# A hybrid decoder step: paced first loads, squares of x on VectorE, and the third norm in pairs of blocks

## The chip, the cores and the metric

The kernel runs on one core of one Trainium2 chip. The metric is the device time of one execution in microseconds (us); the time of a kernel is the median of its runs. Engines are named as in the profile: PE is TensorE (PEld its weight loads), DVE VectorE, ACT ScalarE, POOL GpSimd, SP SyncE, which here only issues DMAs. Lines (L131) are those of the kernel's file before the change.

## The reference

One inference step of one decoder layer, in fp32, for 256 new prompt tokens and 8 x 8 decode tokens, 320 tokens in all, with a model width of 2048:

```python
h    = rms_norm(x, norm_mix_pre)
proj = h @ w_in                       # 2048 x 9248: gate u, v, SSD z, x/B/C, dt
mix  = concat(gate(u, v), ssd(z, xbc, dt)) @ w_out
x    = x + rms_norm(mix, norm_mix_post)
up   = rms_norm(x, norm_ffn_pre) @ ffn_w_up        # 2048 x 11264
f    = (gelu(conv(g)) * conv(u)) @ ffn_w_down      # g, u: the halves of up
x    = x + rms_norm(f, norm_ffn_post)
rms_norm(x, w) = x * rsqrt(mean(x*x) + 1e-6) * w
```

The gate is a spatial gating unit inside chunks of 128 tokens, the SSD a chunked state-space scan; both lie away from the change. The outputs are x, the SSD states and the last rows that the convolutions read.

## The kernel before, in words

**Layout and products.** Activations lie transposed: 128 features of a block on the partitions, 320 tokens (NT) along the row; x has 16 such blocks (KD). Every fp32 product is made of three single-pass products (`accumulate`, L140 to L142): operands are split in a high half (rounded by ScalarE) and a low half (the rest, by VectorE), and high x high, high x low and low x high are summed in PSUM.

**Weights.** `slab` (L110) loads 128 x 1024 weights (two blocks of 128 rows by 512 columns, or four by 256, or one block by 512 as half a slab) by a DMA on SP's queue into `wraw`, casts them on ScalarE to `whi` (L127) and subtracts on VectorE to `wlo` (L131). Each of the three has three buffers, so a load starts when VectorE is done with the slab three before it. `project` (L164) runs 16 blocks of a projection through four PSUM banks. The first projection (the gate's v, L616) has `small=4`: its first four blocks come one at a time (k0 = 0, 1, 2, 3, two to a buffer), then two at a time (k0 = 4, 6, 8, 10), then four. The very first slab is loaded in two cuts (128 and 384 columns) whose products are made by part (L177): four high x high, four high x low, four low x high.

**The start.** TensorE makes ten products of ones (EARLY, L70) that nobody reads, until the first weights are there. x comes by ScalarE's DMA queue (`load_x`, L554) in pieces: block 0 with the scale column, block 1, blocks 2-3, blocks 4-5 at once, and then two blocks each time an odd block has been split (L574). `x_ready` (L565) splits block by block: `h_hi` on ScalarE (L569), `h_lo` on VectorE (L570). A tiny activation (L561) brings ScalarE's table in before its first cast. The first norm's factor does not stand in front of the products: x's squares are taken beside them (`x_squares`, L576), two blocks at a time on ScalarE (L582), and added to a sum (L584), for kt = 2, 4, 6 on GpSimd and for 8 to 14 on VectorE; the factor is multiplied in afterwards.

**The third norm.** After the output projection, `x1_ready` (L1075) makes the new x block by block (L1081, L1082) and splits it, while `project(ffn_w_up, 0, ...)` (L1089) already multiplies four column blocks of the gate half and, with `more`, two of the other half. When the last of the 16 blocks is made (`added[15]`), the squares of all blocks are taken one by one on ScalarE (L301; the first few earlier) and added one by one on VectorE (L302) into `sq3`. TensorE sums them over the partitions with products by ones (`token_sums`, L278), VectorE takes the inverse root in eleven small steps (`rsqrt_of`, L246), TensorE spreads it over the partitions (`spread`, L287), ScalarE copies it to `r3` (L293). In `ffn_up(0)` (L1104, L1146) another column block, `ps_one`, is multiplied meanwhile: two slabs of eight blocks; the sums are asked for behind the first slab, with a priority that draws them as far forward as their data. With `r3` there the six waiting banks and `ps_one` are evicted (L1122, L1123), and the last column block, `ps_other`, takes the first PSUM bank that comes free.

The second norm uses another root, `rsqrt_by_root` (L263): a sum of two parts, ScalarE's square root (L271), VectorE's reciprocal and one refining step.

**What sets the order.** The kernel is written with a scheduler that orders each engine's instructions ahead of time, by priority among those that its own model holds ready; on the chip each engine and each queue then works strictly in that order. `tc.high_priority(offset)` and `first()` raise a priority; `tc.issue_after(ins)` puts what is issued in the block, on the engine of `ins`, behind `ins`. Buffers of a pool that carry one tag are reused in turn, and a writer waits for the readers of what was there.

Of the kernel before, what the change touches and what calls it, by code (L numbers as in the profile page):

```python
# [9 lines left out]
F32 = mybir.dt.float32  # L10
# [3 lines left out]
ALU = mybir.AluOpType  # L14
# [11 lines left out]
NF = DFF // P  # L26
NH = 32
EPS = 1e-6
EARLY = 10
D_COL = 4 * KD + 120 + 8 * NF  # L30
U0, V0, Z0, X0, B0, C0, DT0 = 0, 2048, 4096, 6144, 8192, 8704, 9216

# [2 lines left out]
def hybrid_step(  # L35
# [71 lines left out]

    slab_load, split_after, both = [], [None], []

    def slab(src, half=0, begins=False):  # L110

        n = src.shape[2]
        with tc.high_priority(offset=100000):
            m = n * src.shape[1]
            if not half:
                both[:] = [wp.tile([P, 1024], F32 if i == 0 else F32R, tag=t, name=t, bufs=3) for i, t in enumerate(("wraw", "whi", "wlo"))]
            raw, hi, lo = (t[:, m * half:m * half + m] for t in both)
            cuts = (slice(0, P), slice(P, m)) if begins else (slice(0, m),)
            if begins:
                for o in cuts:  # L120
                    slab_load.append(sp.dma_start(raw[:, o], src[:, 0, o]).ins)
            else:
                slab_load.append(sp.dma_start(raw.rearrange("p (a n) -> p a n", n=n), src).ins)
            late = split_after[-1]
            with tc.issue_after(late[0]) if late else nullcontext(), tc.issue_after(late[1]) if late else nullcontext():
                for i, o in enumerate(cuts):
                    made = act.copy(hi[:, o], raw[:, o]).ins  # L127
                    if begins and i == 0:
                        with tc.issue_after(made):
                            begins()  # L130
                dve.tensor_tensor(out=lo, in0=raw, in1=hi.bitcast(F32), op=ALU.subtract)  # L131

        def block(k, c):
            o = k * n + c * P
            return hi[:, o:o + P], lo[:, o:o + P]
        return block
# [27 lines left out]
    def project(w, c0, evac, width=512, spare=False, late=None, quiet=0, ready=None, small=0, after=None, ahead=1, rate=1, more=None, held=None):  # L164

        nb = width // P
        ps = [misc(f"ps_{c0}_{j}") if spare else mm.tile([P, 512], F32, tag="mm", name=f"ps_{c0}_{j}") for j in range(nb)]
        if more:
            ps += [misc(f"ps_{c0}_{j}") for j in range(nb, nb + 2)]

        def part(src, k0, nk, js):
            wb = slab(src, k0 % 2 if nk == 1 else 0, (lambda: ready(0, 1)) if ready and k0 == 0 and nk == 1 else False)
            by_part = range(1 if ready and k0 == 0 and nk < 4 else 0)
            for k in by_part:
                for i in (0, 1, 2) if nk == 1 else (0, 2, 1):
                    for c, j in enumerate(js):
                        pe.matmul(ps[j][:, :NT], wb(k, c)[i // 2], hT[i % 2][:, k, :], start=i == 0, stop=False)  # L177
            for c, j in enumerate(js):
                for k in range(len(by_part), nk):
                    kt = k0 + k  # L180
                    part_last[:] = [accumulate(ps[j][:, :NT], wb(k, c), hT[0][:, kt, :], hT[1][:, kt, :], kt == 0, kt == KD - 1)]
                if k0 + nk == KD and late is None:
                    evac(j, ps[j])
            if k0 < KD - quiet:
                for _ in range(rate):
                    tick()
        cuts, k0 = [], 0
        if nb == 4:
            while k0 < KD - 4:
                cuts.append((k0, 1 if k0 < small else 2))  # L190
                k0 += cuts[-1][1]
        cuts += [(k, 4) for k in range(k0, KD, 4)]
        there = None

        for cut in cuts[:ahead] if ready else []:
            there = ready(*cut)
        for i, (k0, nk) in enumerate(cuts):
            with tc.issue_after(there or after) if there or after and i > 1 else nullcontext():
                if ready and i + ahead < len(cuts) and (ahead or i):
                    there = ready(*cuts[i + ahead])  # L200
                if nk < 4:
                    part(rows_of(w, k0, nk, c0, 512), k0, nk, range(4))
                    if more and k0 % 4 == 2:
                        if k0 == 2:
                            split_after.append((rooted[-1], low[1]))
                        with tc.issue_after(held[1]):
                            part(rows_of(w, k0 - 2, 4, more, 256), k0 - 2, 4, (4, 5))
                        split_after.append(None)
                else:
                    for h in range(nb // 2):  # L210
                        part(rows_of(w, k0, 4, c0 + 256 * h, 256), k0, 4, (2 * h, 2 * h + 1))
                    if more:
                        part(rows_of(w, k0, 4, more, 256), k0, 4, (4, 5))
        if late is not None:
            late += [(evac, j, p) for j, p in enumerate(ps)]
# [47 lines left out]
    def rsqrt_by_root(rest, ps, scale, rows=P):  # L263

        v = tp.tile([P, 3], F32, tag="rs_v3", name="rs_v")[:rows]
        r = tp.tile([P, 3], F32, tag="rs_r3", name="rs_r", bufs=3)[:rows]
        t = tp.tile([P, 3], F32, tag="rs_t3", name="rs_t")[:rows]
        s = tp.tile([P, 3], F32, tag="rs_s3", name="rs_s")[:rows]
        dve.tensor_scalar(out=v, in0=rest, scalar1=scale, scalar2=EPS, op0=ALU.mult, op1=ALU.add)
        dve.scalar_tensor_tensor(out=v, in0=ps, scalar=scale, in1=v, op0=ALU.mult, op1=ALU.add)  # L270
        rooted.append(act.activation(s, v, AF.Sqrt).ins)  # L271
        dve.reciprocal(r, s)
        dve.scalar_tensor_tensor(out=t, in0=v, scalar=-0.5, in1=r, op0=ALU.mult, op1=ALU.mult)
        dve.tensor_tensor(out=t, in0=t, in1=r, op=ALU.mult)
        rsqrt_ins.append(dve.scalar_tensor_tensor(out=r, in0=t, scalar=1.5, in1=r, op0=ALU.add, op1=ALU.mult).ins)
        return r
# [110 lines left out]
    with ExitStack() as mctx:  # L387
# [153 lines left out]
        with tc.tile_pool(name="gp", bufs=1) as gp:  # L541
# [13 lines left out]
                cs = slice(KD + NT * k if k else 0, KD + NT * (k + n))  # L555
                act.dma_start(flat[:, cs], xT[:, cs])
            with tc.high_priority(offset=300000):
                for k, n in ((0, 1), (1, 1), (2, 2), (4, 2)):
                    load_x(k, n)
                    if k == 1:  # L560
                        act.activation(held, ones[:, 0:1], AF.Square)  # L561

            x_split = []

            def x_ready(k0, nk):  # L565
                with tc.high_priority(offset=100000):
                    for kt in range(k0, k0 + nk):
                        x = xf[:, kt, :]
                        x_split.append(act.activation(hT[0][:, kt, :], x, AF.Copy, scale=pre[:, kt:kt + 1]).ins)  # L569
                        dve.scalar_tensor_tensor(out=hT[1][:, kt, :], in0=x, scalar=pre[:, kt:kt + 1],  # L570
                                                 in1=hT[0][:, kt, :].bitcast(F32), op0=ALU.mult, op1=ALU.subtract)
                        if kt % 2 and kt < 10:
                            with tc.issue_after(x_split[-1]):
                                load_x(kt + 5, 2)  # L574

            def x_squares():  # L576

                yield from repeat(None, 4)
                for kt in range(0, KD, 2):
                    sq = acc[:, kt:kt + 2, :]  # L580
                    with tc.high_priority(offset=100000):
                        act.activation(sq, xf[:, kt:kt + 2, :], AF.Square)  # L582
                    if kt:
                        (pool if kt < 8 else dve).tensor_tensor(out=acc[:, 0:2, :], in0=acc[:, 0:2, :], in1=sq, op=ALU.add)  # L584
                    if kt not in (8, 12):
                        yield
                with first():
# [142 lines left out]
        with tc.tile_pool(name="sd", bufs=1) as sd:  # L730
# [358 lines left out]
            project(ffn_w_up, 0, None, late=up0, ready=x1_ready, after=behind, ahead=1, more=DFF, held=added)  # L1089
            with tc.issue_after(low[2]):  # L1090
                next(rest[1])
            with tc.issue_after(added[15]):
                for kt in range(KD):
                    add_square(sq3, acc[:, kt, :], kt < 1, dve, ("pv", 4))
    x1 = acc


    with tc.tile_pool(name="fp", bufs=1) as fp:
# [5 lines left out]
        def ffn_up(g):  # L1104
# [41 lines left out]
            if g == 0:  # L1146

                ps = misc("ps_one")
                for i in range(2):
                    wb = slab(rows_of(ffn_w_up, 8 * i, 8, DFF + 256, P))  # L1150
                    for k in range(8):
                        kt = 8 * i + k
                        accumulate(ps[:, :NT], wb(k, 0), hT[0][:, kt, :], hT[1][:, kt, :], kt == 0, kt == KD - 1)
                    if i == 0:
                        with first():
                            r = rsqrt_of(token_sums(sq3), 1.0 / D, 3)
                with first():
                    spread(r, r3)
                up0.append((None, 6, ps))
# [208 lines left out]
```

## Time and profile before

| | |
|---|---|
| time, median of 3 runs (lowest to highest) | 1786.09 us (1786.07 to 1788.71) |
| the profiled execution | 1786.56 us |
| its span, first to last instruction | 1784.9 us |
| DVE, ACT, POOL busy | 1191.5, 799.3, 286.7 us |
| moved by DMA | 289.94 MB, 162 GB/s on average |

A profile row of the timeline has the start in us, the duration in us, engine, line, operation, tiles written and read, partitions x elements, and the count of instructions that it joins; in brackets the idle time of the engine before it and what ended it. A row of the waits has who waited, on which line, for what; then us in all, times, and the longest. A row of the chain has start, us and what. A row of one line's instructions has count, then shortest, median and longest in ns, and the first and last start. A row of issues has count, size of one, and the us from issue to landing. The durations of matmuls overlap, since they are pipelined; their starts tell the pace.

### The profile page before, as it was taken

Reading aid. Unit: us, or ns where it says so; the run is one execution under the profiler, and the core shown is the slowest. Engines: PE = TensorE matmul, PEld = TensorE weight load, DVE = VectorE, ACT = ScalarE, POOL = GpSimd, SP = SyncE. Lnnn points to the kernel's source line nnn. Section 1 sums busy time; section 2 is a strip of 40 time slices with the busy share of each in tenths; the row PEclk is TensorE's granted clock in tenths of the full one; section 3 lists DMA queues with packets and bytes.
Section 4 is the critical chain, followed back from the end, with each engine's and each line's share of the span. In section 5 each row is a group of like instructions: output and inputs, shape, how many; then the busy total and the mean of one; then the engine's idle time right before and its main releaser. Section 6 shows DMA issues by size and latency. Waiting matters only on the chain.

```text
span 1784.9 us, 31254 instructions
## 1 busy us (share of the span) xinstructions
PE 1774.2 (99%) x12230; PEld 1743.2 (98%) x12230; DVE 1191.5 (67%) x2077; ACT 799.3 (45%) x1121; POOL 286.7 (16%) x601
## 2 busy tenths in 40 slices
PE   9999999999999999999999999999999999999998
PEld 9999999999999898999999999999999999999998
DVE  7459664556987869677875474756566575656575
ACT  6443455334444445445555333343434343433445
POOL 3104200000431303103121010110101020101004
PEclk9999999999999999999999999999999999999999
DMA  7646544456665565554554555454454545454443
GB/s 231 186 141 200 163 138 154 154 154 184 203 207 185 175 205 179 154 171 146 177 158 149 150 154 153 146 155 150 150 153 152 148 156 151 149 153 153 147 155 107
DMA packets 221699, 289.94 MB, mean 162 GB/s; under 512 B 16368, under 2 KB 151152, under 8 KB 221360
## 3 DMA queue, kind: packets, MB, share of 16 engines
q1 hardware_dynamic: 209824, 268.74, 49.7%
q10 hardware_dynamic: 10016, 14.16, 2.3%
q0 software_dynamic: 1712, 5.05, 0.9%
q8 instruction: 96, 1.57, 0.4%
q14 instruction: 51, 0.42, 0.1%
HBM read 273.08 MB, written 14.82 MB: 161 GB/s over the span
## 4 chain that ended last, share of the span: by engine, by line
PE 94%; issue 2%; DVE 1%; DMA 1%; POOL 0%; ACT 0%; POOLq 0%; SPq 0%; DVEq 0%; ACTq 0%
PE ps L140 20%; PE ps L141 20%; PE ps L142 20%; PE pd L140 10%; PE pd L142 10%; PE pd L141 10%; PE y_ps L946 1%; DMA wraw<-in_w_in 1%; PE yo_ps L851 1%; PE up_ps L868 1%; DVE wlo L131 0%; PE sg L694 0%; PE xt_ps L380 0%; PE vt_ps L600 0%; PE tsum L283 0%
## 5 line engine op out<-in xcount | busy, mean ns | idle before, releaser
L131 DVE TENSOR_TENSOR wlo<-wraw,whi 128x1024 fp32r<-128x1024 f32 (+1 forms) x474 | 582.3, 1229 | 411.0 <-ACT whi L127 409.0
L127 ACT CAST whi<-wraw 128x1024 fp32r<-128x1024 f32 (+1 forms) x475 | 494.8, 1042 | 714.5 <-PE ps L141 416.3
L140 PE MATMUL ps<-h_hi,whi 128*128 128x320 f32 x2520 | 782.5, 311 | 1.4 <-DVE pad L405 0.8
L141 PE MATMUL ps<-h_lo,whi 128*128 128x320 f32 x2520 | 779.1, 309 | 0.8 <-DVE h_lo L570 0.8
L142 PE MATMUL ps<-h_hi,wlo 128*128 128x320 f32 x2520 | 778.6, 309 | 0.2 <-DVE wlo L131 0.2
L140 PEld LDWEIGHTS ps<-h_hi,whi 128*128 128x128 f32 x2520 | 473.5, 188 | 4.8 <-issue 2.8
L141 PEld LDWEIGHTS ps<-h_lo,whi 128*128 128x128 f32 x2520 | 473.7, 188 | 2.8 <-issue 1.1
L142 PEld LDWEIGHTS ps<-h_hi,wlo 128*128 128x128 f32 x2520 | 473.4, 188 | 0.9 <-DVE wlo L131 0.4
L140 PE MATMUL pd<-fhi,whi 128*128 128x320 f32 x704 | 217.4, 309 | 0.0
L141 PE MATMUL pd<-flo,whi 128*128 128x320 f32 x704 | 217.3, 309 | 0.0
L142 PE MATMUL pd<-fhi,wlo 128*128 128x320 f32 x704 | 217.3, 309 | 0.0
L140 PE MATMUL pd<-ohi,whi 128*128 128x320 f32 x448 | 140.7, 314 | 0.0
L142 PE MATMUL pd<-ohi,wlo 128*128 128x320 f32 x448 | 139.1, 310 | 0.0
L141 PE MATMUL pd<-olo,whi 128*128 128x320 f32 x448 | 138.9, 310 | 0.0
L142 PEld LDWEIGHTS pd<-fhi,wlo 128*128 128x128 f32 x704 | 132.3, 188 | 0.0
L141 PEld LDWEIGHTS pd<-flo,whi 128*128 128x128 f32 x704 | 132.3, 188 | 0.0
L140 PEld LDWEIGHTS pd<-fhi,whi 128*128 128x128 f32 x704 | 132.3, 188 | 0.0
L1134 POOL COPY ptf<-pad 128x2 f32<-128x2 f32 x88 | 21.0, 239 | 610.0 <-DVE pad L1122 609.3
L237 DVE TENSOR_TENSOR acc_ffn<-acc_ffn,pd 128x320 f32<-128x320 f32 (+1 forms) x161 | 77.6, 483 | 38.2 <-PE pd L142 36.8
L140 PEld LDWEIGHTS pd<-ohi,whi 128*128 128x128 f32 x448 | 84.2, 188 | 2.0 <-issue 1.1
L141 PEld LDWEIGHTS pd<-olo,whi 128*128 128x128 f32 x448 | 84.2, 188 | 0.4 <-issue 0.2
L142 PEld LDWEIGHTS pd<-ohi,wlo 128*128 128x128 f32 x448 | 84.2, 188 | 0.4 <-issue 0.3
(309 smaller groups left out, 1613.9 us busy)
## 6 DMA issues: line engine op xcount, KB each, us to landing
wraw<-in_ffn_w_up SPq DMA_DIRECT2D x176, 512.0 KB, 3.7
wraw<-in_w_in SPq DMA_DIRECT2D x144, 512.0 KB, 3.8
wraw<-in_ffn_w_down SPq DMA_DIRECT2D x88, 512.0 KB, 3.3
wraw<-in_w_out SPq DMA_DIRECT2D x64, 512.0 KB, 3.4
st<-in_state_ssm SPq DMA_DIRECT2D x32, 256.0 KB, 4.2
out_ssm_state_sample<-st ACTq DMA_DIRECT2D x30, 256.0 KB, 2.9
cs<-dacs_d SPq DMA_DIRECT2D x16, 320.0 KB, 4.5
xr<-in_xT SPq DMA_DIRECT2D x4, 640.0 KB, 4.0
```

The lines of the kernel that those rows point to most:

```text
L127: made = act.copy(hi[:, o], raw[:, o]).ins
L131: dve.tensor_tensor(out=lo, in0=raw, in1=hi.bitcast(F32), op=ALU.subtract)
L140: pe.matmul(ps, whi, xhi, start=first, stop=False)
L141: pe.matmul(ps, whi, xlo, start=False, stop=False)
L142: return pe.matmul(ps, wlo, xhi, start=False, stop=last).ins
L237: added_last[:] = [dve.tensor_tensor(out=acc[:, nb, ts], in0=acc[:, nb, ts], in1=ps[:, ts], op=ALU.add).ins]
L851: pe.matmul(ps_yo[row:row + 32, :256], cms[:, 4 * h + i, :], st[h][:, 256 * r:256 * r + 256], start=i == 0, stop=i == 3, tile_position=(0, ...
L868: made = pe.matmul(ps, bm[:, h], xsp[:, h], start=True, stop=True)
L946: pe.matmul(ps[64 * i:64 * i + 64, cols], w(hl), x(hl, m, cpx), tile_position=(0, 64 * i), **flags)
L1134: pool.tensor_copy(ptf[:, k, :], pad[:, 256:258])
```

## The change

Six edits, at two places. At the start: eight idle products for ten; the slabs of k0 = 3 and k0 = 4 of the first projection get a small VectorE copy into their load buffer, from the first column of the high half of block 0 and of block 1, so that the load waits for that split; the load of x's blocks 2-3 is issued behind the small activation, that of blocks 4-5 behind the split of block 0; all adds of x's squares are VectorE's. At the third norm: the squares are taken of two blocks at a time, into four parts of two buffers that had held x, and added in pairs behind the fourteenth block (`added[13]`), with one last add of the two halves of the pair; the sums are asked for behind the fifth block of `ps_one`, at the earliest; and the inverse root is the one by ScalarE, of one sum (`rest` is None) instead of two.

```diff
-EARLY = 10
+EARLY = 8
...
-    def slab(src, half=0, begins=False):
+    def slab(src, half=0, begins=False, paced=None):
...
+            if paced is not None:
+                dve.tensor_copy(raw[:, 0:1], paced)
             if begins:
...
+        begun = []
+
         def part(src, k0, nk, js):
-            wb = slab(src, k0 % 2 if nk == 1 else 0, (lambda: ready(0, 1)) if ready and k0 == 0 and nk == 1 else False)
+            wb = slab(src, k0 % 2 if nk == 1 else 0, (lambda: ready(0, 1)) if ready and k0 == 0 and nk == 1 else False,
+                      begun[k0 - 3] if small and k0 in (3, 4) else None)
+            if k0 < small:
+                begun.append(wb(0, 0)[0][:, 0:1].bitcast(F32))
...
     def rsqrt_by_root(rest, ps, scale, rows=P):
...
-        dve.tensor_scalar(out=v, in0=rest, scalar1=scale, scalar2=EPS, op0=ALU.mult, op1=ALU.add)
-        dve.scalar_tensor_tensor(out=v, in0=ps, scalar=scale, in1=v, op0=ALU.mult, op1=ALU.add)
+        dve.tensor_scalar(out=v, in0=ps if rest is None else rest, scalar1=scale, scalar2=EPS, op0=ALU.mult, op1=ALU.add)
+        if rest is not None:
+            dve.scalar_tensor_tensor(out=v, in0=ps, scalar=scale, in1=v, op0=ALU.mult, op1=ALU.add)
...
             with tc.high_priority(offset=300000):
-                for k, n in ((0, 1), (1, 1), (2, 2), (4, 2)):
-                    load_x(k, n)
-                    if k == 1:
-                        act.activation(held, ones[:, 0:1], AF.Square)
+                load_x(0, 1)
+                load_x(1, 1)
+                table = act.activation(held, ones[:, 0:1], AF.Square).ins
+                with tc.issue_after(table):
+                    load_x(2, 2)
...
-                        if kt % 2 and kt < 10:
+                        if kt == 0 or kt % 2 and kt < 10:
                             with tc.issue_after(x_split[-1]):
-                                load_x(kt + 5, 2)
+                                load_x(kt + 5 if kt else 4, 2)
...
-                        (pool if kt < 8 else dve).tensor_tensor(out=acc[:, 0:2, :], in0=acc[:, 0:2, :], in1=sq, op=ALU.add)
+                        dve.tensor_tensor(out=acc[:, 0:2, :], in0=acc[:, 0:2, :], in1=sq, op=ALU.add)
...
-            with tc.issue_after(added[15]):
-                for kt in range(KD):
-                    add_square(sq3, acc[:, kt, :], kt < 1, dve, ("pv", 4))
+
+            room = [op.tile([P, 4, NT], F32, tag="xs", name="sq_two", bufs=2) for _ in range(2)]
+            total, *some = [t[:, i:i + 2, :] for t in room for i in (0, 2)]
+            for i, kt in enumerate(range(0, KD, 2)):
+                sq = some[i % 3] if i else total
+                act.activation(sq, acc[:, kt:kt + 2, :], AF.Square)
+                if i:
+                    with tc.issue_after(added[13]):
+                        dve.tensor_tensor(out=total, in0=total, in1=sq, op=ALU.add)
+            dve.tensor_tensor(out=sq3, in0=total[:, 0, :], in1=total[:, 1, :], op=ALU.add)
...
-                        accumulate(ps[:, :NT], wb(k, 0), hT[0][:, kt, :], hT[1][:, kt, :], kt == 0, kt == KD - 1)
-                    if i == 0:
-                        with first():
-                            r = rsqrt_of(token_sums(sq3), 1.0 / D, 3)
+                        made = accumulate(ps[:, :NT], wb(k, 0), hT[0][:, kt, :], hT[1][:, kt, :], kt == 0, kt == KD - 1)
+                        if kt == 4:
+                            with first(), tc.issue_after(made):
+                                r = rsqrt_by_root(None, token_sums(sq3), 1.0 / D)
```

## The prediction

> **What bounds the kernel now.** I read the page first (span, busy shares, chain), then TensorE's own waits, then the timeline around each wait that this change can reach.
>
> ```profile
> span 1784.9 us, 31254 instructions
> PE 1774.2 (99%) x12230; PEld 1743.2 (98%) x12230; DVE 1191.5 (67%) x2077; ACT 799.3 (45%) x1121; POOL 286.7 (16%) x601
> PE 94%; issue 2%; DVE 1%; DMA 1%; POOL 0%; ACT 0%; POOLq 0%; SPq 0%; DVEq 0%; ACTq 0%
> ```
>
> ```profile
> PE ps L141 <- DVE h_lo L570: 0.8, 1, 0.8
> ...
> PE tsum L283 <- DVE sq L302: 0.7, 1, 0.7
> ...
> PE ps L140 <- ACT whi L127: 0.6, 1, 0.6
> ...
> PE ps L142 <- DVE wlo L131: 0.2, 1, 0.2
> ```
>
> TensorE (PE) is busy in 99% of the span and is 94% of the chain. The change removes none of its products but two idle ones, so it can only win where TensorE stands. The second fence is the whole of what it can win by: four waits of 0.8, 0.7, 0.6 and 0.2 us, the first, third and fourth in the first projection, the second at the third norm. Whatever engine gets lighter elsewhere is beside TensorE and worth nothing.
>
> **Part 1: the first products.** The rows are TensorE's and ScalarE's timeline of the first microseconds, then one row of the chain of waits, and the issues with their size and us to landing: the two cuts of the first slab, the third load of x, the fifth slab, and the median of all slabs of this matrix.
>
> ```profile
> 1.13 4.40 PE L70 MATMUL early<-ones 128*128 128x128 f32 x20 [1.13 <-DVE ones L66]
> 3.04 0.20 ACT L561 ACTIVATE held<-ones 128x1 f32<-128x1 f32 x1
> 4.83 0.51 ACT L127 CAST whi<-wraw 128x384 fp32r<-128x384 f32 x1 [0.35 <-DMA wraw<-in_w_in]
> 5.29 0.84 PE L177 MATMUL ps<-h_hi,whi 128*128 128x320 f32 x4
> 6.54 0.75 PE L177 MATMUL ps<-h_hi,wlo 128*128 128x320 f32 x4
> 7.23 0.62 ACT L127 CAST whi<-wraw 128x512 fp32r<-128x512 f32 x1 [1.42 <-DMA wraw<-in_w_in]
> 7.90 0.42 PE L140 MATMUL ps<-h_hi,whi 128*128 128x320 f32 x1 [0.60 <-ACT whi L127]
> 8.88 0.31 PE L140 MATMUL ps<-h_hi,whi 128*128 128x320 f32 x1
> ```
>
> ```profile
> 1.73 5.48 DMA wraw<-in_w_in
> ```
>
> ```profile
> wraw<-in_w_in SPq DMA_DIRECT2D x1, 64.0 KB, 2.5
> wraw<-in_w_in SPq DMA_DIRECT2D x1, 192.0 KB, 3.6
> vt<-in_xT ACTq DMA_DIRECT2D x1, 320.0 KB, 5.6
> wraw<-in_w_in SPq DMA_DIRECT2D x1, 512.0 KB, 7.0
> ...
> wraw<-in_w_in SPq DMA_DIRECT2D x144, 512.0 KB, 3.8
> ```
>
> *Two idle products fewer.* 20 records (two to a product) take 4.40 us, so two products are 4/20 of that, 0.9 us. But only the first of the four real products could use it: the other three need the second cut of the weights, whose split ends at 4.83 + 0.51 = 5.34, and TensorE starts the second of the four at about 5.5 today. Bounds 0 and 0.9; I take **0.1**, next to the split's row.
>
> *The paced loads.* Steady products stand 0.147 apart (four in 0.75 us, the last lasting 0.31: 0.44 / 3). The last of the first block starts at 6.54 + 3 x 0.147 = 6.98; unhindered, the fourth product of the second block would start 0.59 later, at 7.57. It starts at 8.88: **1.30 us lost**, because the second slab, issued at 1.73, lands at 7.21 and is split from 7.23. Its companion is the third load of x (320 KB, issued beside it, 5.6 us to landing). The change issues that one only behind the activation that ends at 3.24 (about 1.5 us later) and after the third slab, holds the fourth slab until the first split, and holds the fifth (512 KB; 7.0 us today) until the second split. So the second slab shares the DMA engines with far less. TensorE wants its high half at about 7.1; the split takes 0.62, so landing by 6.4 wins all. From an issue at 1.73 that is 4.7 us; the two cuts ahead of it landed in 2.5 and 3.6, and with fewer rivals for the bandwidth I expect about 4.3. Bounds 0 (it lands as today) and 1.30; I take **1.1**.
>
> The pacing adds two VectorE copies of 128x1, in the place of a load that used to leave at once. Nearest rows: VectorE's 128x3 operations, 0.16 each. The first waits for the cast of the first cut, which lies before the product at 5.29; until the first split of x VectorE has nothing else to do. The second waits for the second slab's cast; behind it stand that block's own splits, ready at the same moment, so 0.16 is its price. Behind both on SP's queue stand all later slabs: the fourth leaves at about 4, the fifth at about 7. The fifth is wanted three blocks of 12 products after the second block's start, 7.1 + 3 x 1.76 = 12.4; with today's 7.0 us it lands at 14, with the usual 3.8 at 11. This is the new risk (rival A). ScalarE issues the moved x loads in gaps in which it waits for weights anyway.
>
> **Part 2: x's squares.**
>
> ```profile
> 16.27 1.23 DVE L131 TENSOR_TENSOR wlo<-wraw,whi 128x1024 fp32r<-128x1024 f32 x1 [2.41 <-ACT whi L127]
> 17.41 1.56 POOL L584 TENSOR_TENSOR acc_mix<-acc_mix 128x640 f32<-128x640 f32 x1 [11.91 <-ACT acc_mix L582]
> 17.41 2.37 DVE L570 SCALAR_TENSOR_TENSOR h_lo<-vt,h_hi 128x320 fp32r<-128x320 f32 x2
> 18.26 0.31 PE L142 MATMUL ps<-h_hi,wlo 128*128 128x320 f32 x1
> 19.37 0.41 PE L141 MATMUL ps<-h_lo,whi 128*128 128x320 f32 x1 [0.80 <-DVE h_lo L570]
> ```
>
> ```profile
> L570 DVE SCALAR_TENSOR_TENSOR h_lo<-vt,h_hi x16: 537/546/1904, 4.5 to 28.5; 128x320 fp32r<-128x320 f32 x16
> ```
>
> ```profile
> L584 DVE TENSOR_TENSOR acc_mix<-acc_mix x4: 817/821/826, 29.0 to 35.5; 128x640 f32<-128x640 f32 x4
> ```
>
> A GpSimd add and a split of x start together at 17.41; of the 16 such splits the median takes 0.55, the longest 1.90, and it is this one, for while the add runs VectorE crawls. TensorE waits for it: 19.37 - 18.26 is 1.11 between starts instead of 0.147, and 0.1 more at the restart: **1.07 lost**. With no add on GpSimd the split takes 0.55 and the wait has no cause. VectorE takes three adds at 0.82 = 2.5 us, low in priority, and gets back 1.35 from this split alone. Bounds: 1.07 won, or the adds stand in front of splits (rival C). I take **0.9**, since TensorE will come here a microsecond or more earlier and the sixth and seventh blocks' weights may then be a little late.
>
> **Part 3: the third norm.**
>
> ```profile
> 12.04 0.72 ACT L582 ACTIVATE acc_mix<-vt 128x640 f32<-128x640 f32 x1
> ```
>
> ```profile
> 868.75 2.07 DVE L302 TENSOR_TENSOR sq<-sq,sq 128x320 f32<-128x320 f32 x4
> ...
> 879.63 1.08 DVE L302 TENSOR_TENSOR sq<-sq,sq 128x320 f32<-128x320 f32 x2
> ```
>
> ```profile
> 879.71 0.31 PE L140 MATMUL ps_one<-h_hi,whi 128*128 128x320 f32 x1
> 880.76 0.83 PE L283 MATMUL tsum<-ones,sq 128*128 128x1 f32 x6 [0.74 <-DVE sq L302]
> 881.46 0.39 PE L141 MATMUL ps_one<-h_lo,whi 128*128 128x320 f32 x1
> ```
>
> The 15 adds (four in 2.07, so 0.5 each, 7.6 us) run from 868.75 to 880.71; the other 4.4 us are weight splits of 1.23 and small waits. The sums stand one product into the block and wait 0.74 for them. By pairs: 7 adds at 0.82 (the same shape, line 584) and one at 0.5 make 6.2 us, and two or three splits fall among them: done at 868.75 + 6.2 + 3 x 1.23 = 878.6 at the latest, about 877.5 with two. A pair's square takes 0.72 of ScalarE, 5.8 us in all, and three buffers let it run ahead of the adds. The sums now stand behind the fifth block, at 879.71 + 15 x 0.147 = 881.9: over 3 us of slack. The 0.74 goes; their own time (0.8) stays.
>
> ```profile
> 833.49 0.15 DVE L269 TENSOR_SCALAR rs_v<-tsum 128x3 f32<-128x3 f32 x1
> ...
> 834.79 0.16 DVE L275 SCALAR_TENSOR_TENSOR rs_r<-rs_t,rs_r 128x3 f32<-128x3 f32 x1
> ```
>
> ```profile
> 884.62 0.16 DVE L257 SCALAR_TENSOR_TENSOR rs_r<-rs_t,rs_r 128x3 f32<-128x3 f32 x1
> ...
> 887.19 0.42 DVE L1122 TENSOR_TENSOR pad<-ps,r 128x256 f32<-128x256 f32 x1
> ```
>
> ```profile
> L140 PE MATMUL ps_other<-h_hi,whi x16: 307/308/310, 888.9 to 895.5; 128*128 128x320 f32 x16
> ```
>
> Sums later means the root later, but the root by ScalarE's square root (second norm's rows) takes 833.49 to 834.95, 1.5 us: from 882.7 it is there at 884.2, against 884.78 by today's eleven steps. What is late next is the PSUM buffer: the last up-block's products start at 888.9, a microsecond earlier after the change, and need the first eviction (887.19 + 0.6). That leaves 0.2 us or more. The new pair buffers are those of x's blocks, free after the last x add; the next stage's first loads might wait for them on SP's queue, which I cost at nothing, since the slab behind them is for the products from 888.9, ten us after the last add. I take **0.85**: 0.74 and a tenth at the spread; bounds -0.9 (every later step waits) and 1.0.
>
> **Sum.** 0.1 + 1.1 + 0.9 + 0.85 = 2.95; for some waits surviving as fractions I take off 0.15: **2.8 us**. The profiled execution took 1786.56 us (span 1784.9 and 1.7 around it): 1783.8. The median of the runs is 1786.09, 0.5 under it: **1783.3**.
>
> **The clock, weighed.**
>
> ```profile
> 835.10 0.51 PE L291 MATMUL spread<-ident,rs_r 128*128 128x128 f32 x3 [0.42 <-DVE rs_r L275]
> ```
>
> Three 128x128 records of the same kind fit in 0.51 there; the 20 at the start stand twice as far apart. So TensorE runs at half speed until about 5.3 and the first real products then go at full rate. With eight idle products it stands idle from 4.6 to 5.4. If half speed then holds through the first block, that costs 12 x 0.147 = 1.8 us (rival B). The Trainium skill, page "TensorE: Matmul & The Clock Gate", section "Part 1: The HAM clock gate", says that full clock follows a busy window of about 3.4 us which runs free of the kernel. By that rule a missed window is an estimated 3.4 / 2 = 1.7 us; no run here yet shows whether a short hole spoils it.
>
> **Rivals.**
> - **A, pacing gives back what it wins.** The fifth slab lands at 13 or later and TensorE stands at the fifth block, or the second slab lands as today. For it: 7.0 us to landing today. Against: most of that was queueing. Only parts 2 and 3 stay: 1786.1 - 1.8 = 1784.3, up to 1785.
> - **B, the clock comes one block later:** 1783.3 + 1.8 = 1785.1. For it: the hole; against: three quarters of the warm-up is unchanged.
> - **C, slower: the adds on VectorE.** VectorE works in order. If an add stands in front of a weight split while its square is not done, all splits wait: GpSimd got its square at 17.41, so the split at 16.27 would begin at 17.41 + 0.82 = 18.2, 2.0 us late; three adds, 6.0. Against that stand the wins 0.1 + 1.1 + 0.85 and the 1.07 that it replaces: net +2.9, 1789.0; and as each late split also frees its load buffer late, up to 1791. It decides from about 1.05 us an add, on TensorE's path. For it: GpSimd idled 11.9 us for such a square. Against: the splits have high priority, the adds none, and the four adds already on VectorE stall nothing.
> - **D, it doesn't do what it says at the third norm:** the sums no longer wait, but the root, the spread or the eviction does, for as long. Then 1783.3 + 0.85 = 1784.2.
>
> **How the numbers follow.** Forecast 0.55 (own range 1782.2 to 1784.4), A 0.13, B 0.08, C 0.13, D 0.11. About 0.2% (3.6 us) is what a measurement of this kernel can tell from no change: faster is below 1782.5, slower above 1789.7. Nearly everything must come true for faster, since the waits sum to 1.30 + 1.07 + 1.0 + 0.1 to 0.9; I give 0.18, out of the forecast's best part. Slower is the worse half of C and a share for an order of instructions that shifts elsewhere: 0.09. The rest, 0.73, is within. The range 1781.8 to 1787.5 takes in A, B, D and the mild half of C.
>
> **What would show it.** Right: in TensorE's waits the rows on lines 570, 127 and 131 of the start are gone; the second slab lands before 6.5; no GpSimd add beside a split of x, and the longest such split below 0.7; the sums of the third norm show no wait for a square and follow 15 products. Wrong: a new TensorE wait for a cast at 12 to 13 us (A), products 0.29 apart after 5.4 (B), splits of weights waiting behind adds of 128x640 between 14 and 26 us (C), a wait at the spread or at the last up-block near 888 (D); or a wait of a microsecond at a line that the change doesn't touch.

## The result, and the profile after

The changed kernel took 1793.24 us in the median of 6 runs (1790.74 to 1794.68), the kernel before 1786.24 on the same chip: a ratio of 1.0033, 95% interval [1.0023, 1.0043]. It became slower, by about 0.3%; the forecast was 1783.3 and the range ended at 1787.5. The profiled execution took 1792.21. On another chip the same program gave 1790.26 against 1787.39, ratio 1.0007 [0.9997, 1.0017]; that interval takes in no change. (A ratio is not simply the quotient of the two medians; in the runs below the two differ by up to 0.001.)

The page's head and its chain after the change, then TensorE's waits (us in total, times, longest):

```profile
span 1790.5 us, 31228 instructions
PE 1774.9 (99%) x12226; PEld 1743.8 (97%) x12226; DVE 1186.3 (66%) x2069; ACT 799.6 (45%) x1114; POOL 280.5 (16%) x598
PE 95%; DVE 2%; DMA 1%; ACT 0%; issue 0%; POOL 0%; SPq 0%; POOLq 0%; DVEq 0%; ACTq 0%
```

```profile
PE ps L142 <- ACT whi L129: 4.9, 2, 3.9
PE ps L142 <- DVE pad L413: 1.4, 1, 1.4
...
PE ps L142 <- DVE acc_mix L244: 0.6, 1, 0.6
```

The shares are nearly the same; the waits tell the story. The waits for h_lo (0.8), for the second slab's low half (0.2) and for the third norm's squares (0.7) are gone. In their place stands one wait of 3.9 us for a cast of weights, in the first projection. The other wait on that line, for the second slab, is 1.0 us, where it was 0.6 before. The chain of waits in the first 30 us (start, us, what) says what the cast waited for:

```profile
1.73 5.78 DMA wraw<-in_w_in
7.53 0.63 ACT whi L129
...
9.38 7.39 DMA wraw<-in_w_in
16.85 1.05 ACT whi L129
17.95 0.56 PE ps L142
18.51 0.27 PE ps L143
```

The fifth block's slab (k0 = 4) leaves at 9.38, takes 7.39 us to land, is cast, and TensorE starts on it at 17.95; its products then follow each other by 0.27 us, not by 0.147. The timeline around it, engine by engine:

```profile
1.74 1.28 ACT L568 ACT_TABLE_LOAD   x1 [1.74 <-PEq L1375]
1.80 0.39 ACTq L564 DMA_DIRECT2D vt<-in_xT  x1
3.03 0.20 ACT L568 ACTIVATE held<-ones 128x1 f32<-128x1 f32 x1
...
3.82 0.33 SPq L125 DMA_DIRECT2D wraw<-in_w_in  x1
...
8.18 0.69 DVE L133 TENSOR_TENSOR wlo<-wraw,whi 128x512 fp32r<-128x512 f32 x1 [1.60 <-ACT whi L129]
8.79 0.14 DVE L120 COPY wraw<-whi 128x1 f32<-128x1 f32 x1
8.90 0.38 SPq L125 DMA_DIRECT2D wraw<-in_w_in  x1
9.38 0.41 SPq L125 DMA_DIRECT2D wraw<-in_w_in  x1
...
13.72 0.31 PE L144 MATMUL ps<-h_hi,wlo 128*128 128x320 f32 x1
16.85 1.04 ACT L129 CAST whi<-wraw 128x1024 fp32r<-128x1024 f32 x1 [5.64 <-DMA wraw<-in_w_in]
17.95 0.56 PE L142 MATMUL ps<-h_hi,whi 128*128 128x320 f32 x1 [3.91 <-ACT whi L129]
```

Two loads leave SP's queue at 8.90 and 9.38, and the one that TensorE needs next is the second. The first is the load of the *seventh* block (k0 = 6): it takes over the first slab's buffer, which the subtraction of 8.18 to 8.87 sets free, and in the order of instructions built for SP it stands one place ahead of the load for k0 = 4. In the kernel before the fifth block's load left at 3.60 and the seventh's at 8.60, in this order:

```profile
3.60 0.38 SPq L123 DMA_DIRECT2D wraw<-in_w_in  x1
...
8.60 0.38 SPq L123 DMA_DIRECT2D wraw<-in_w_in  x1
```

The paced copy, which must come before the load of k0 = 4, stands on VectorE behind that same subtraction.

By stretch of 2 us (busy us and instructions of PE, PEld, DVE, ACT, POOL; granted clock; DMA share; GB/s), after the change:

```profile
8.00:10.00 2.00, 1.78 (x10) 1.52 (x11) 1.76 (x6) 1.92 (x5) 0.00 (x0) 1.00 0.70 203
...
14.00:16.00 2.00, 0.04 (x1) 0.00 (x0) 0.00 (x0) 0.00 (x0) 0.00 (x0) 1.00 1.04 395
16.00:18.00 2.00, 0.05 (x1) 0.06 (x1) 0.07 (x1) 1.15 (x2) 0.00 (x0) 1.00 0.32 121
18.00:20.00 2.00, 2.00 (x8) 2.00 (x9) 1.66 (x3) 2.00 (x4) 0.00 (x0) 0.51 0.77 182
20.00:22.00 2.00, 2.00 (x11) 2.00 (x10) 2.00 (x3) 2.00 (x4) 0.00 (x0) 0.63 0.93 330
```

and before it, at the same place:

```profile
8.00:10.00 2.00, 1.84 (x11) 1.57 (x12) 1.94 (x5) 1.91 (x5) 0.00 (x0) 1.00 1.02 399
```

From 8 to 10 us the DMA engines now run at 0.70 where they were full: the held-back load leaves them idle, and the same bytes are missing later, when they are full at 1.04 with TensorE standing. Behind the stand the clock is granted at 0.51 and 0.63 for about 3.4 us.

The rest of the change works. All 16 splits of x (h_lo) take 0.54 to 0.55 us, where one took 1.90, and the third norm's sums wait for nothing (first the group of splits with its shortest, median and longest in ns, then the timeline):

```profile
L579 DVE SCALAR_TENSOR_TENSOR h_lo<-vt,h_hi x16: 539/542/551, 4.1 to 30.4; 128x320 fp32r<-128x320 f32 x16
```

```profile
882.84 0.49 DVE L1110 TENSOR_TENSOR sq<-sq_two 128x320 f32<-128x320 f32 x1
887.58 0.72 PE L291 MATMUL tsum<-ones,sq 128*128 128x1 f32 x6
```

**Where the 5.6 us of the span came from.** TensorE runs the same 11,398 products of 320 columns in all these kernels, in nearly the same order, so the start of the n-th product can be compared in two timelines. The table gives how many us later than in the kernel before the product at that place starts (negative: earlier), for this kernel and the experiments that follow. Each row is a single execution, the profiled one, so small differences between rows can be chance: e2's and e9's are the fastest of their eleven, e6's is the slowest.

| kernel | at 12 us | 30 | 440 | 600 | 860 | 1000 |
|---|---|---|---|---|---|---|
| after | +0.16 | +4.81 | +5.45 | +5.66 | +5.66 | +4.60 |
| after, run again | -0.65 | +3.56 | +3.69 | +2.69 | +2.70 | +1.66 |
| e6 queue order mended | -0.07 | +0.11 | +0.73 | +3.01 | +3.02 | +1.96 |
| e4 paced by the first cast | +0.63 | -0.43 | +0.03 | +0.67 | +0.62 | -0.43 |
| e2 no pacing | -0.25 | -1.32 | -1.44 | -1.43 | -1.43 | -2.49 |
| e3 pacing alone | +0.06 | +5.14 | +5.04 | +4.79 | +4.78 | +6.96 |
| e7 x's third load truly later | +0.49 | -0.57 | -0.73 | -1.45 | -1.41 | -2.47 |
| e9 that load halved | +0.78 | -0.29 | -0.07 | -0.75 | -0.72 | -1.78 |
| e8 18 idle products | +0.16 | +3.12 | +3.65 | +3.91 | +3.95 | +2.89 |
| e10 10 idle products | +0.38 | +3.41 | +6.07 | +6.97 | +6.96 | +5.90 |
| third norm alone | +0.23 | +0.19 | +0.33 | -0.59 | -0.54 | -1.50 |
| x adds alone | 0.00 | -1.06 | -1.14 | +1.67 | +1.73 | +2.05 |

For the first row: 0.16 at 12 us; 5.88 once the fifth block is through (stand 17.95 - 13.72 - 0.147 = 4.08, half clock about 1.6); less 1.07 as the h_lo wait is gone: 4.81. Small waits in untouched code (pad 0.59 more, two near 508 and 523 of 1.35 together, one near 588 of 1.14 gone) make 5.66; the third norm takes off 1.06, which leaves 4.60. The last 1.05 of the span lie behind the last product, where the last store of the output takes 3.5 us to land for 2.9 before. In the other executions this tail is 0 to 1.6 us longer than before; what sets it is open.

### The profile page after: what moved, and what is told of

Its sections match the earlier page's. It is cut to its first block, busy times and chain, and to the rows that moved or that the text cites. A ratio compares the mean times of both kernels' runs of the same rounds, so it can differ in the third digit from the quotient of the medians.

```text
span 1790.5 us, 31228 instructions
## 1 busy us (share of the span) xinstructions
PE 1774.9 (99%) x12226; PEld 1743.8 (97%) x12226; DVE 1186.3 (66%) x2069; ACT 799.6 (45%) x1114; POOL 280.5 (16%) x598
## 4 chain that ended last, share of the span: by engine, by line
PE 95%; DVE 2%; DMA 1%; ACT 0%; issue 0%; POOL 0%; SPq 0%; POOLq 0%; DVEq 0%; ACTq 0%
PE ps L142 20%; PE ps L143 20%; PE ps L144 20%; PE pd L142 10%; PE pd L144 10%; PE pd L143 10%; DMA wraw<-in_w_in 1%; PE y_ps L955 1%; DVE wlo L133 1%; PE yo_ps L860 1%; PE up_ps L877 0%; PE sg L703 0%; DMA cs<-dacs_d 0%; PE xt_ps L388 0%; PE vt_ps L609 0%
```

## The experiments

The theory (T1 in the expectations): the paced load was put behind another load on SP's queue; that order makes the fifth block stand, and the stand drops the clock. Rivals: any such wait makes the block late, whatever the order (T2); the loss is in the shifted order of later work (T3).

**e6: the order alone.**

```
-                slab_load.append(sp.dma_start(raw.rearrange(...), src).ins)
+                with tc.issue_after(slab_load[-1]) if len(slab_load) == 6 else nullcontext():
+                    slab_load.append(sp.dma_start(raw.rearrange(...), src).ins)
```

> The kernel after, with one edit: the load of the seventh block's slab (k0 = 6) must stand behind that of the fifth's (k0 = 4) on SP's queue. The paced copy stays as it is, on VectorE behind the second slab's splits. T1 (the queue's order is the cause: the load of k0 = 6 leaves first at 8.90 and takes the DMA engines): the slab of k0 = 4 leaves at about 8.9, lands at about 13.5 (4.8 us, as the load of k0 = 6 had it in the kernel after), TensorE stands some 1.0 to 1.3 us in place of 4.1, the granted clock does not fall, and the time is 4 to 4.8 us under the kernel after, 1.5 to 2.5 us over the kernel before. T2 (the wait on the second cast is too late in any order): landing at 15 or later, 1 to 2 us under the kernel after at most. T3 (the loss is not at the start but in the order of later work, by the x adds or the third norm): no more than 1 us under the kernel after.

Measured: 1786.59 (1.0001 [0.9993, 1.0010]), span 1787.8. Its chain:

```profile
8.73 4.55 DMA wraw<-in_w_in
13.36 1.05 ACT whi L130
14.46 0.41 PE ps L143
```

The load waits for the same copy and leaves as late as before, at 8.73 for 9.38, but first, and lands in 4.55 us for 7.39. TensorE's stand shrinks from 4.08 to 0.82, the clock stays at 1.00, and the offset at 30 us falls from +4.81 to +0.11. So the order is worth 4.7 us; the lateness of the paced load by itself costs 0.82. T2 falls.

**e4: both copies paced by the first cast.** `begun[k0 - 3]` becomes `begun[0]`.

> The kernel after, but the fifth block's slab (k0 = 4) is paced by the first cast, as the fourth is, in place of the second cast. Both copies stand on VectorE ahead of the first split. T1: both loads leave at about 4.6 in the right order, the slab of k0 = 4 lands at 10 to 11 as in the kernel before, TensorE does not stand at the fifth block and the clock stays up; the wins of the x adds and the third norm remain: 1 to 2 us under the kernel before, 7 to 9 under the kernel after. T2 (any pacing of this load makes the fifth block late): the wait at the fifth block stays above 2 us, the time above the kernel before. T3: not under the kernel before.

Measured: 1787.31 (0.9999 [0.9990, 1.0008]). The fifth block's load left at 4.08, in the right order, landed at 11.41, and no product waited for it. But the time only came level: the second slab landed at 7.98 (7.21 before), TensorE's clock came late (see the last section), and later waits took 1.1. T1 is right about the stand, and was too hopeful by 1 to 2 us on the rest.

**e2: no pacing.** The argument `paced` is None everywhere; the rest of the change stays.

> The kernel after without either paced copy; the moved loads of x, the adds on VectorE, the eight idle products and the third norm stay. T1 and T2: no wait at the fifth block, 1.5 to 2 us under the kernel before (x adds 1.0, third norm 1.0, less what later waits take back). T3: at or over the kernel before.

Measured: 1786.19 (0.9995 [0.9987, 1.0004]), profiled span 1782.8, 2.1 under the one of before. By its trace it is 1.32 earlier at 30 us and 2.49 at 1000. The runs cannot tell it from the kernel before, and put it under the changed kernel.

**e3: pacing alone on the kernel before.**

> The kernel before with the two paced copies alone. On SP's queue the load of k0 = 6 stands ahead of that of k0 = 4, as in the kernel after. T1 and T2: TensorE stands 3.5 to 4.2 us at the fifth block, the granted clock falls for some 3.4 us after it, and the time is 4 to 6 us over the kernel before: more than the whole change loses. T3: within 1 us of the kernel before.

Measured: 1790.13 (1.0019 [1.0009, 1.0029]), span 1791.8. Its chain:

```profile
9.13 8.11 DMA wraw<-in_w_in
17.32 1.05 ACT whi L129
18.41 0.64 PE ps L142
```

The copies alone reproduce the stand (4.64) and the half clock behind it. The wait at the third norm, where nothing was edited, grew from 0.7 to 1.2, and the clock falls to half a second time behind it (see the last section): together most of the 2.18 us between 860 and 1000 in the table. The median is 3.0 over the kernel before, a little less than expected; the profiled execution, 1793.51, is the third slowest of its eleven.

**e7: x's third load truly behind the activation.** Without pacing; the activation writes one column of that load's place, so the load must wait for it.

```
-                table = act.activation(held, ones[:, 0:1], AF.Square).ins
+                table = act.activation(xf[:, 2, 0:1], ones[:, 0:1], AF.Square).ins
```

> The kernel after without the paced copies, and with the small activation writing its one column into x's third load's own place, so that this load has to wait for it; in the kernel after it only stands behind it on the queue and left at 1.80 all the same. The load should leave at about 3.3. T1, as the prediction's second step has it (the second slab lands late because x's third load shares the DMA engines): the second slab lands at about 6.3, 0.8 us under the 7.07 of the kernel without pacing, and if the third load of x is still there by 9, the time falls by some 0.5 us against that kernel. Rival R4 (the DMA engines are full from 2 us on and share among all that has been issued, so the third and fourth slabs take the place of that load): landing at 7 or later, and no gain; or the third block of x comes late and costs up to 1 us.

Measured: 1786.54 (0.9990 [0.9981, 0.9999]), span 1782.8. Two stretches of its timeline:

```profile
6.14 0.63 ACT L129 CAST whi<-wraw 128x512 fp32r<-128x512 f32 x1
7.01 0.75 PE L184 MATMUL ps<-h_hi,wlo 128*128 128x320 f32 x4
7.59 0.31 PE L142 MATMUL ps<-h_hi,whi 128*128 128x320 f32 x1
...
9.21 0.31 PE L144 MATMUL ps<-h_hi,wlo 128*128 128x320 f32 x1
10.11 0.41 PE L142 MATMUL ps<-h_hi,whi 128*128 128x320 f32 x1 [0.59 <-ACT whi L129]
```

The load left at 3.26 and the second slab landed at 6.12, against 7.07 in e2: the prediction's mechanism is real, and the second block follows without a wait. But x's load lands at 8.96, and TensorE waits at the third block instead (10.11 - 9.21 - 0.147 = 0.75). The wait moved. As T1 feared and R4 said, there is no gain against e2.

**e9: that load cut in two of 160 KB,** the second behind the first.

> The kernel without pacing whose third load of x truly waits for the activation, with that load cut in two of 160 KB, the second behind the first. The first half should land at 8.0 to 8.3 in place of 8.96, so the wait of 0.75 at the third block goes, and the second block is met without a wait as there: 0.3 to 0.7 us under that kernel by the trace, 2 to 3 us under the kernel before. Rival R4 (the DMA engines are full, so any order only moves the wait): another wait of the same size at the third or fourth block, no gain.

Measured: 1786.81 (0.9997 [0.9989, 1.0006]). The first half landed at 9.17, not at 8.0 to 8.3. No product waited for it, but the clock came at 9.5 us in this execution, the first block ran at half speed, and TensorE reached the third block only at 10.97; so it says nothing on halving.

**e8 and e10: TensorE kept busy while it stands,** with 18 and with 10 idle products ahead of the fifth block.

```
+            if small and k0 == 4 and nk == 2:
+                idle = misc("idle")
+                with tc.issue_after(part_last[0]):
+                    for _ in range(18):
+                        made = pe.matmul(idle[:, :P], ones, ones, start=True, stop=True).ins
```

> The kernel after, with 18 idle products of 128x128 (0.22 us each) between the fourth and the fifth block, to be run while TensorE stands there. If the fall of the granted clock is a consequence of standing idle: the stand at the fifth block's first product remains (about 13.7 to 17.9), the granted clock stays at 1.00 from 18 to 22 us, the next products stand 0.147 apart in place of 0.267, and the time is 1.4 to 1.7 us under the kernel after. If the clock falls for another reason, or if its fall is hidden by the waits for later slabs: within 0.3 us of the kernel after, or slower by what the idle products overrun.

> The kernel after with 10 idle products (2.2 us) between the fourth and fifth block, fewer than the stand is long, so that they can't overrun it. The stand for the fifth slab stays (first product at about 16.5 to 18), the idle time left is 2 us at most and the granted clock should stay at 1.00. If standing idle is what drops the clock, this saves the same 1.6 us as 18 idle products did; the time lies 3 to 4 us over the kernel before, 1.5 under the kernel after. If 10 are too few, the clock falls to 0.5 at some 18 us as in the kernel after.

Measured: e8 1791.12 (1.0015 [1.0006, 1.0024]), e10 1793.11 (1.0022 [1.0011, 1.0033]). TensorE in e8, and the stretch behind with its clock:

```profile
13.88 4.18 PE L184 MATMUL idle<-ones 128*128 128x128 f32 x36
17.81 0.40 PE L142 MATMUL ps<-h_hi,whi 128*128 128x320 f32 x1
```

```profile
18.00:20.00 2.00, 2.00 (x16) 2.00 (x15) 1.66 (x3) 2.00 (x4) 0.00 (x0) 1.00 0.62 147
```

The fifth block starts nearly as late as in the changed kernel (17.81 - 13.73 - 0.147 = 3.93 lost, for 4.08), yet the clock stays at 1.00 and the stretch from 18 to 20 us has 16 products where it had 8. The offset behind the block is 4.19 for 5.88. Of these 1.69 us the shorter stand is 0.15, so the half clock costs about 1.5 us, and standing idle is its cause. In e8 the slab had landed at 15.56 and the idle products overran by about a microsecond. Ten did not overrun and held the clock there too (+3.41 at 30 us), but that execution lost 2.65 us more at another place, told in the last section, so its total came out over the expectation.

**Third norm alone,** and **x's adds on VectorE alone,** on the kernel before.

> The kernel before with the third norm's part alone (pairs of squares, sums behind the fifth block, root by ScalarE). As predicted: no wait for the sums, 0.85 to 1.0 us under the kernel before, and nothing moved ahead of 860 us. Rival T3: this part is what brings the waits near 159, 504 and 520 us of the kernel after, and it ends at or over the kernel before.

> The kernel before with x's squares added by VectorE alone. As predicted: the split of x at 17.4 takes 0.56 in place of 1.90, its wait of 0.8 is gone, 0.9 to 1.07 us less at 30 us. Rival T3: the order of VectorE's work shifts behind it, the waits near 159 (pad), 504 (the add into acc_mix) and 520 us appear here, and take back 0.6 to 1.5 us.

Measured: 1786.27 (0.9991 [0.9982, 1.0000]) and 1787.21 (0.9995 [0.9986, 1.0004]). In the trace each edit does what it should where it acts: the third norm 1.06 (-0.54 to -1.50 in the table, -0.44 just ahead of it), x's adds 1.06 at 30 us. But the second lost three times as much again between 480 and 520 us, in code that it does not touch. Of TensorE's waits these lie mostly there (0.9 each); a third, for the squares of the third norm, grew from 0.7 to 1.1:

```profile
PE y_ps L946 <- DVE cs L935: 1.1, 2, 0.9
...
PE ps L140 <- DVE acc_mix L237: 0.9, 1, 0.9
```

**The changed kernel again.**

> The kernel after, unchanged, beside the two below on one chip, to tell what in its trace comes back and what is chance. T1: the stand of about 4 us at the fifth block, the half clock behind it and the lost wait at the third norm come back in the same size; the waits near 159, 504, 519 and 588 us, which came and went in the other kernels by 0.5 to 1.3 us, need not. 4 to 6 us over the kernel before. T3: those waits come back in the size of the first trace (1.4 at the pad, 0.6 at the add into acc_mix, none at 588).

Measured: 1790.26, span 1787.6. Its longest wait:

```profile
PE ps L142 <- ACT whi L129: 3.7, 1, 3.7
```

The stand comes back (3.9 us between products beyond the usual step), and the half clock; the wait for acc_mix does not, and the pad's is 0.9 for 1.4. From 30 to 860 us the first execution lost 0.85 and this one won 0.86, with the same program. So the program alone does not fix those waits, and T3 falls as the main cause. What decides them is open. The ratio, too, is smaller on this chip than in the first measurement; the traces show 4.60 and 1.66 us at 1000 us, of which 1.7 are those waits and 1.25 the start.

## Why the prediction was wrong

**The step that failed** is the one on the paced loads: "The second waits for the second slab's cast", "Behind both on SP's queue stand all later slabs: the fourth leaves at about 4, the fifth at about 7", and with it the landing "at 14, with the usual 3.8 at 11". The fourth left at 3.82. The fifth left at 9.38 and landed at 16.77, for three reasons, each in a row above: the second cast ran from 7.53, not from 6.4; the copy stood behind the 0.69 of the low half; and one load was let past it. The prediction took the order on SP's queue as given, and an edit to a wait had changed that order. Its sum had no term for a stand at the fifth block: it took the 1.1 us of the second slab in full and left the fifth to rival A. The fifth slab then took 7.39 to land, as a second 512 KB load behind another, with DMA engines full; e6 gives 4.55 for the same load ahead of it.

**Rival A** named the right mechanism ("TensorE stands at the fifth block") and had the wrong price. It only took back the 1.1 us that pacing was to win, 1784.3 up to 1785, and left out the stand itself (4.08) and the clock (about 1.6). Its own numbers would already have shown a loss: landing at 14 and a cast of 1.05 put the first product at 15.1, against a need at 12.4, so 2.7 us on the slow side. Measured were 17.95 against 13.87. The chance of 0.09 for slower lay in rival C, which did not happen (a split of weights came behind an add by up to 0.6 us, near 28 us, and TensorE waited for none), and in "an order of instructions that shifts elsewhere", which came nearest but had no place and no price.

**The second slab** was to land at 6.4 and win 1.1. It landed at 7.51, no earlier than the 7.21 of before, since the third load of x still left at 1.80, in the middle of the table load: standing behind an activation on ScalarE's queue is not waiting for it. In the eleven executions where that load left at 1.8 us the second slab landed at 6.69 to 7.98 (6.69 in the second one of the changed kernel); in e7 and e9, where it does wait, at 6.12 and 6.47, so the mechanism was right. But e7 could not win the 1.1 even so: the wait went to the next block. The DMA engines are full early on (a share of 0.94 to 1.04 in each 2 us from 2 to 10 before the change), and in e7 the choice of the load that goes first only chose where to wait.

**Two idle products fewer:** 0.1 forecast, nothing measured (+0.16 at 12 us, no more than other executions vary by); no run has this edit alone.

**x's adds:** 0.9 forecast; between the fifth block and 30 us 1.06 to 1.07 were won in nine of the ten executions that have them on VectorE, 0.82 in e6. But e3, which has them on GpSimd, won 1.06 there too. Adds and splits still ran side by side in it (three pairs of splits took 2.3 to 2.4 us each, the longest split 1.92), but TensorE came 5 to 6 us late and waited for none of them. So the runs without the stand, x's adds alone and e2, show what the edit is worth; in the changed kernel the stand would probably have hidden that wait anyway.

**Third norm:** 0.85 forecast, 1.05 to 1.07 in all ten executions that have it, a little over the upper bound of 1.0. Rival D did not come: the sums stand at 887.58, 4 us behind the last add.

**The clock:** rival B looked for it at the first products, where eight idle products do leave a hole (TensorE waits 0.32 us at 5.44); it struck at the fifth block. The page "TensorE: Matmul & The Clock Gate" of the Trainium skill, section "Part 1: The HAM clock gate", says that an idle window of about 3.4 us halves the clock. The trace agrees here: a stand of 4.08, then 0.51 and 0.63 granted for some 3.4 us. Two shorter stands were followed by half clock as well (last section).

## What to carry to other kernels

A load that is held back is not delayed alone: ask which loads of its queue will now be issued ahead of it, and price the landing with those in front and the DMA engines full. If an edit adds a wait, look at the order of the queue that was built, not at the order in the source. When a rival's mechanism is "the engine stands", its price is the stand and what the stand does to the clock, not the gain that was hoped for.

## What the runs showed of the hardware

A stand of about 2 us can drop the clock. In e10 TensorE stood 2.23 us between two products near 163 us, and the clock followed:

```profile
162.76 0.31 PE L142 MATMUL ps<-h_hi,whi 128*128 128x320 f32 x1
164.99 0.41 PE L142 MATMUL ps<-h_hi,whi 128*128 128x320 f32 x1 [1.92 <-DVE pad L418]
```

```profile
164.00:166.00 2.00, 1.01 (x4) 1.04 (x5) 1.93 (x5) 2.00 (x6) 2.00 (x10) 0.80 0.73 212
166.00:168.00 2.00, 2.00 (x9) 2.00 (x9) 1.77 (x4) 1.16 (x2) 0.34 (x1) 0.50 0.41 124
```

The stands of 1.63 to 1.69 us at the same place in the changed kernel, e6 and e8 left it at 1.00. But length alone does not decide. In e3, at the third norm, 1.53 us between two starts, with six small sums behind, were followed by half clock from 888.51 to 891.92:

```profile
884.84 0.31 PE L142 MATMUL ps_one<-h_hi,whi 128*128 128x320 f32 x1
886.37 0.83 PE L290 MATMUL tsum<-ones,sq 128*128 128x1 f32 x6 [1.23 <-DVE sq L309]
887.06 0.39 PE L143 MATMUL ps_one<-h_lo,whi 128*128 128x320 f32 x1
```

```profile
890.00:892.00 2.00, 2.00 (x9) 1.96 (x9) 0.32 (x2) 0.00 (x0) 0.00 (x0) 0.52 0.82 258
```

From the last full product to the next that is 2.22 us. With x's adds alone the same place took 2.06 us, in the kernel before 1.75, and both kept 1.00. What the rule is, these runs don't show.

The clock's arrival at the start varies: full by the trace's clock records from 4.4 us (the changed kernel, e2) over 7.2 (e4) to 9.5 us (e9), and with the ten idle products of before from 4.5 (e3) to 6.7 (x's adds alone). In e9 the first block's products are 0.27 apart where they are 0.147 in the kernel before:

```profile
7.90 1.27 PE L184 MATMUL ps<-h_hi,wlo 128*128 128x320 f32 x4
```

So rival B does happen. The same program had full clock from 4.4 us in one execution and from 6.2 in the other (the changed kernel, run again), so part of it is chance; nine executions with eight idle products and four with ten are too few to say whether their number matters.
